# A gate table in DRAM, filled by indexed DMA and read back, in place of one-hot matmuls

## The chip, the cores and the metric

One core of a Trainium2 chip runs the kernel as one program. The metric is the device time of an execution in microseconds (us). The engines work side by side: TensorE (PE, matrix products), VectorE (DVE), ScalarE (ACT), GpSimd (POOL) and SyncE (SP, which here starts most DMAs). Each takes its instructions in one fixed order, and an instruction that waits holds up all that are queued behind it on its engine.

## The reference

Two transformer blocks over 256 tokens of width 2048, in float32. The part around the change is the expert layer (PEER) of the first block. Each token picks, for each of 8 heads, 16 of 16384 experts by two searches over 128 keys each, and every expert has a row `u` and a row `v`:

```python
s = jnp.einsum('thpd,hpnd->thpn', q, sub_keys)
s_half, i_half = lax.top_k(s, PEER_TOPK)                  # 16 of 128, twice per head
cand = s_half[:, :, 0, :, None] + s_half[:, :, 1, None, :]
cand_idx = i_half[:, :, 0, :, None] * PEER_NKEYS + i_half[:, :, 1, None, :]
top_s, pos = lax.top_k(cand, PEER_TOPK)                   # 16 of 256
idx = jnp.take_along_axis(cand_idx, pos, axis=-1)
g = jax.nn.softmax(top_s, axis=-1)
...
a = jnp.einsum('cd,ced->ce', xc, expert_u[ic])
w = (gc * jax.nn.gelu(a)).astype(xc.dtype)
y = jnp.einsum('ce,ced->cd', w, expert_v[ic])
```

So a token has 8 x 16 = 128 picks (with repetitions over the heads, whose gates add up).

## The kernel before

Rather than gather `u`, the kernel computes a token's product with all experts, in 128 blocks of 128 experts, and multiplies by a table of gates that is zero where an expert isn't picked. `w0` and `w1` hold, for each block, 128 experts by 256 tokens. Every float32 product is split in a high and a low part, and three products of the halves are summed.

`stat_block` (L905) is one block: two units of 512 KB (`raw`, loaded by SP), each split by ACT into `hi` (L155) and by DVE into `lo` (L157), and on PE one 512-column matmul (L915, the last one of the block L918) and one of 256 columns (L916) for each of 16 steps. ACT copies half of the result (`rest`, L923), DVE adds it (L924). `raw`, `hi` and `lo` have three buffers each. DVE's order holds the `lo`s between its other work.

`route` (L1204) runs 16 such blocks over the query weights, and behind each the searches (`top16`, L927) on DVE: MAX8, FIND_INDEX8 and MATCH_REPLACE8 over 128 columns for both halves of the tokens, and behind every second block over 256 columns of `cand` (L1233). In between `renorm` scales the input for the expert blocks in four parts: `rn` on POOL (L1198) and DVE (L1199), `xt` on DVE (L1201). Then it works out the two indices and the gate of each pick and transposes them with six PE transposes (L1269 to L1271) into `i1T`, `i2T` and `gT`.

`peer_blocks` (L937) runs the 128 expert blocks. The first 25 (NPARK) only store gelu of the product. In the next 64 each block carries four tokens' gates: `onehots` (L975, L978, DVE) makes for each token two one-hot matrices, one with the gates in it, and a fp32 matmul of the two (L1019, PE) gives the token's 128 x 128 table. `place` multiplies it into the blocks that are done (L991) and stores it for the others (L993), `note` marks the experts in use, and `finish` multiplies a later block by its gates. Then `rank` numbers the experts in use, and the 127 sends of L1034 (indirect DMA, POOL) write the used rows in a compact list, from which `peer_v` gathers `v` (L1159, POOL).

A tile framework sorts every engine's instructions by priority when the program is made; its order is fixed then. A DMA that POOL starts uses one of eight lanes in turn, and waits for the one eight before it.

## Time and profile before

| | |
|---|---|
| median of three runs | 3036.33 us (3036.22 to 3039.43) |
| profiled execution | 3041.31 us, its span 3039.6 us |
| granted TensorE clock, mean | 0.99 |
| busy, share of the span | PE 98%, DVE 67%, ACT 51%, POOL 13% |
| the expert layer's first product | about 419 to 1190 us of the span |

A share of busy time is a mean over the whole span, so the stages have to be read one by one. Where a group of rows is a timeline, its columns are start (us), duration (us), engine, line, operation, what is written and read, and in brackets the idle time before it and what ended that. A row of the windows view gives a stretch, its length, the busy time of PE, PEld (weight loads), DVE, ACT and POOL (with the number of their instructions), the granted TensorE clock as a share of full speed, the DMA engines' busy share and GB/s.

### The profile page before, as it was taken

The numbers are of one execution on the slowest core, as the hardware profiler recorded it, in microseconds if no ns is written. First come the engines' busy times: TensorE is split into PE (matmuls) and PEld (weight loads), VectorE is DVE, ScalarE is ACT, GpSimd is POOL, SyncE is SP. The second block draws the span as 40 slices with busy tenths as digits, with TensorE's granted clock in tenths as the row PEclk, the third lists the DMA queues.
The fourth block names the chain that finished last, engine by engine and source line by source line (L and its number), as shares of the span: only waits on it lengthen the run. The fifth ranks groups of instructions, "written<-read, shape, count | busy, mean of one in ns | idle before, by whom it ended". The sixth has DMA issues, their size and how long they took to land.

```text
span 3039.6 us, 42009 instructions
## 1 busy us (share of the span) xinstructions
PE 2977.8 (98%) x15470; PEld 2522.4 (83%) x15471; DVE 2021.4 (67%) x3213; ACT 1552.3 (51%) x2409; POOL 393.3 (13%) x403
## 2 busy tenths in 40 slices
PE   8999999999999999998998999999999999999998
PEld 6877888888888887887886888888887888888887
DVE  7776899888888555665667644555656555555555
ACT  5555655454554444565666444555445544444444
POOL 3130102100000674221221000000120000000000
PEclk9999999999999999999999999999999999999999
DMA  6434555544444898876887555555574555555554
GB/s 204 149 132 143 190 188 175 172 166 161 162 164 167 257 285 263 287 285 249 289 293 268 181 192 181 173 170 182 171 243 158 189 191 188 190 192 194 194 194 166
DMA packets 168502, 607.88 MB, mean 200 GB/s; under 512 B 20672, under 2 KB 36096, under 8 KB 154464
## 3 DMA queue, kind: packets, MB, share of 16 engines
q1 hardware_dynamic: 142272, 461.95, 45.2%
q0 software_dynamic: 26016, 143.17, 13.0%
q8 instruction: 123, 2.02, 0.3%
q14 instruction: 91, 0.75, 0.1%
HBM read 581.96 MB, written 23.07 MB: 199 GB/s over the span
## 4 chain that ended last, share of the span: by engine, by line
PE 45%; issue 4%; DMA 1%; POOL 1%; DVE 1%; ACT 0%; POOLq 0%; DVEq 0%; ACTq 0%; SPq 0%
PE mm L915 7%; PE mm L181 7%; PE mm L180 7%; PE mm L182 7%; PE mm L916 4%; PE mm L1107 2%; PE mm L1109 2%; PE mm L1108 2%; POOL vr L1159 1%; PE at L1109 1%; PE at L1107 1%; PE tr L1107 1%; PE at L1108 1%; PE tr L1109 1%; PE tr L1108 1%
## 5 line engine op out<-in xcount | busy, mean ns | idle before, releaser
L157 DVE TENSOR_TENSOR lo<-raw,hi 128x1024 fp32r<-128x1024 f32 (+2 forms) x852 | 1047.7, 1230 | 558.8 <-ACT hi L155 555.7
L155 ACT ACTIVATE hi<-raw 128x1024 fp32r<-128x1024 f32 (+2 forms) x852 | 894.1, 1050 | 624.0 <-PE mm L182 265.0
L915 PE MATMUL mm<-xt,hi 128*128 128x512 f32 x3120 | 1124.9, 399 | 1.1 <-DVE xt L205 1.1
L916 PE MATMUL mm<-xt,lo 128*128 128x256 f32 x3328 | 904.0, 282 | 5.2 <-DVE lo L157 5.1
L915 PEld LDWEIGHTS mm<-xt,hi 128*128 128x128 f32 x3120 | 587.5, 188 | 113.9 <-DVE xt L205 1.5
L916 PEld LDWEIGHTS mm<-xt,lo 128*128 128x128 f32 x3328 | 628.8, 189 | 22.4 <-DVE lo L157 7.6
L181 PE MATMUL mm<-lo,xt 128*128 128x512 f32 (+2 forms) x928 | 363.3, 392 | 0.3 <-DVE lo L157 0.2
L182 PE MATMUL mm<-hi,xt 128*128 128x512 f32 (+2 forms) x928 | 356.1, 387 | 0.0
L157 DVE TENSOR_TENSOR lo<-vr,hi 128x1024 fp32r<-128x1024 f32 x206 | 253.4, 1235 | 137.8 <-ACT hi L155 132.6
L180 PE MATMUL mm<-hi,xt 128*128 128x512 f32 (+2 forms) x928 | 335.0, 391 | 4.9 <-ACT hi L155 2.8
L155 ACT ACTIVATE hi<-vr 128x1024 fp32r<-128x1024 f32 x206 | 216.3, 1055 | 143.8 <-PE mm L1109 122.2
L923 ACT ACTIVATE rest<-mm 128x256 f32<-128x256 f32 x208 | 80.0, 385 | 368.7 <-PE mm L918 368.6
L1108 PE MATMUL mm<-lo,wh 128*128 128x512 f32 x560 | 219.0, 391 | 0.0
L1109 PE MATMUL mm<-hi,wl 128*128 128x512 f32 x560 | 218.6, 391 | 0.0
L180 PEld LDWEIGHTS mm<-hi,xt 128*128 128x128 f32 x928 | 174.9, 190 | 40.4 <-ACT hi L155 3.4
L181 PEld LDWEIGHTS mm<-lo,xt 128*128 128x128 f32 x928 | 176.3, 190 | 35.5 <-DVE lo L157 2.0
L182 PEld LDWEIGHTS mm<-hi,xt 128*128 128x128 f32 x928 | 175.7, 190 | 32.8 <-DVE xt L205 0.4
L1107 PE MATMUL mm<-hi,wh 128*128 128x512 f32 x560 | 157.9, 394 | 15.7 <-ACT hi L155 13.4
L924 DVE TENSOR_TENSOR mm<-mm,rest 128x256 f32<-128x256 f32 x208 | 88.8, 427 | 95.3 <-ACT rest L923 95.2
L1034 POOL DMA_INDIRECT wD<-w,rank x127 | 137.9, 1086 | 77.9 <-DVE bad L1092 21.0
L1159 POOL DMA_INDIRECT vr<-in_peer_v,wr x103 | 96.7, 939 | 329.5 <-DVE lo L157 295.5
L1107 PEld LDWEIGHTS mm<-hi,wh 128*128 128x128 f32 x560 | 105.6, 190 | 39.8 <-ACT hi L155 15.7
(484 smaller groups left out, 3700.9 us busy)
## 6 DMA issues: line engine op xcount, KB each, us to landing
raw<-in_peer_u SPq DMA_DIRECT2D x256, 512.0 KB, 3.3
raw<-in_w_in SPq DMA_DIRECT2D x184, 512.0 KB, 3.2
raw<-in_w_up SPq DMA_DIRECT2D x128, 512.0 KB, 3.2
raw<-in_w_down SPq DMA_DIRECT2D x128, 512.0 KB, 3.5
raw<-in_w_out SPq DMA_DIRECT2D x64, 512.0 KB, 3.3
raw<-in_peer_w_q SPq DMA_DIRECT2D x32, 512.0 KB, 3.5
wr<-wD SPq DMA_DIRECT2D x103, 128.5 KB, 3.5
raw<-in_w_branch_a SPq DMA_DIRECT2D x16, 512.0 KB, 3.2
```

The source lines that it names most:

```text
L155: nc.scalar.activation(hi[:, :n], raw[:, :n], AF.Copy)
L157: nc.vector.tensor_tensor(lo[:, :n], raw[:, :n], hi[:, :n].bitcast(F32), op=ALU.subtract)
L180: mm(o, sh, wh, start=(k == 0), stop=False)
L181: mm(o, sh, wl, start=False, stop=False)
L182: mm(o, sl, wh, start=False, stop=(k == nk - 1))
L915: mm(out, wh, x.both(k), start=(k == 0), stop=False)
L916: mm(out[:, S:], wl, x.hi(k), start=False, stop=False)
L1034: nc.gpsimd.indirect_dma_start(lots[b], bass.IndirectOffsetOnAxis(ap=rank[:, b:b + 1], axis=0), store(b, b + 1)[:, 0, :], None)
L1107: mm(o, sh, vh, start=first, stop=False)
L1108: mm(o, sh, vl, start=False, stop=False)
L1109: mm(o, sl, vh, start=False, stop=last)
L1159: nc.gpsimd.indirect_dma_start(v, None, a["peer_v"], bass.IndirectOffsetOnAxis(ap=w[:, S:ROW].bitcast(U32), axis=0))
```

## The change

The gates go through a table `gD` in DRAM, of 128 blocks x 128 experts x 256 tokens. At the route's start POOL clears it with 16 DMAs of 1 MB from a zeroed part of `w0`. The picks stay with the tokens on the partitions (`eid`, `gate`), so the transposes fall away. For every pick p, DVE sums the gates of all picks of the token with the same expert (`gates`: one operation over 128 x 128 with a sum), and POOL writes the 128 sums of the 128 tokens with one indirect DMA to their cells (128 rows of 4 bytes; a repeated pick goes to a spare block): 2 x 128 indirect DMAs. When all are written, POOL fetches the table into the tiles: blocks 80 to 111 (LATE to RING) into their own place by 8 DMAs of 512 KB, the blocks that are done by DMAs of 256 KB (two blocks) into the free place of blocks 112 to 127, eight at a time. The done blocks are multiplied there in pairs, on POOL or DVE, and `used` finds the experts in use by a maximum on DVE or by sums on ACT. Blocks 25 to 79 store gelu alone, the later ones multiply in `finish`.

```diff
-TPB = 4
-USE = 16
+PICKS = 6
+MARK = 16.0
+GATED = 76
+LATE = 80
+RING = 112
...
-            i1T = gp.tile([P, S], F32, name="i1T")
-            i2T = gp.tile([P, S], BF16, name="i2T")
-            gT = gp.tile([P, S], F32, name="gT")
-            um = gp.tile([P, N0], F32, name="um")
+            eid = gp.tile([P, 2, P], F32, name="eid")
+            gate = gp.tile([P, 2, P], F32, name="gate")
...
-            def onehots(gw):
...
-            def place(blk, ps):
...
-            def note():
...
+            spots = dram_disjoint_views(self.gD, 2 * P)
+            blocks = self.gD[:NBLK * P * S].rearrange("(b p s) o -> b p (s o)", p=P, s=S)
+            todo = [(t, p) for t in range(2) for p in range(0, P, PICKS)]
...
+            def gates():
+                t, p0 = todo.pop(0)
+                ps = range(p0, min(p0 + PICKS, P))
+                for p in ps:
+                    nc.vector.scalar_tensor_tensor(same, ids2[t][:, p:p + P], eid[:, t, p:p + 1], gate2[t][:, p:p + P],
+                                                   op0=ALU.is_equal, op1=ALU.mult, accum_out=total[:, t, p:p + 1])
+                sl = slice(p0, ps.stop)
+                nc.vector.scalar_tensor_tensor(skip[:, t, sl], total[:, t, sl], MARK, skip[:, t, sl],
+                                               op0=ALU.is_ge, op1=ALU.mult)
+                nc.vector.tensor_tensor(place[:, t, sl], cell[:, t, sl], skip[:, t, sl], op=ALU.add)
+                for p in ps:
+                    nc.gpsimd.indirect_dma_start(spots[t * P + p],
+                                                 bass.IndirectOffsetOnAxis(ap=place[:, t, p:p + 1], axis=0),
+                                                 total[:, t, p:p + 1], None)
+
+            def used(v, b, act):
+                if act:
+                    for i in range(2):
+                        for t in range(2):
+                            j = self.junk.tile([P, P], BF16, name="junk", tag="rest", bufs=2)
+                            nc.scalar.activation(j, v[:, i, t * P:(t + 1) * P], AF.Copy,
+                                                 accum_out=um[:, t, b + i:b + i + 1])
+                    return
+                nc.vector.tensor_reduce(um[:, :, b:b + 2], v.rearrange("p b (t s) -> p t b s", t=2), axis=AX.X, op=ALU.max)
 
...
             blk = NPARK
-            with tc.tile_pool(name="gw", bufs=4, reuse_waits="tile") as gw:
-                while done < S:
-                    gps = self.bank("at")
-                    oh = onehots(gw)
-                    def fill(i):
-                        nc.tensor.matmul(gps[:, i * P:(i + 1) * P], oh[i][0], oh[i][1], start=True, stop=True)
-                    ps = self.stat_block(x, a["peer_u"][blk], fill=fill)
-                    place(blk, gps)
-                    if done % USE == 0:
-                        note()
-                    finish(blk, ps)
-                    blk += 1
+            def block():
+                nonlocal blk
+                finish(blk, self.stat_block(x, a["peer_u"][blk]))
+                blk += 1
+            with tc.tile_pool(name="gw", bufs=1, reuse_waits="tile") as gw:
+                um = gw.tile([P, 2, NBLK], F32, name="um")
+                pairs()
+                while todo:
+                    gates()
+                    block()
+                def fetch(b, n, at):
+                    nc.gpsimd.dma_start(store(at, at + n)[:, :, :S], blocks[b:b + n].rearrange("b p s -> p b s"))
+                for b in range(LATE, RING, 4):
+                    fetch(b, 4, b)
+                early = list(range(0, LATE, 2))
+                late = list(range(LATE, NBLK, 2))
+                got, slot = [], RING
+                def load():
+                    nonlocal slot
+                    for _ in range(3):
+                        if early:
+                            b = early.pop(0)
+                            fetch(b, 2, slot)
+                            got.append((b, slot))
+                            slot = slot + 2 if slot + 2 < NBLK else RING
+                load()
+                while blk < GATED:
+                    block()
+                while got or late:
+                    now = list(got)
+                    got.clear()
+                    if early:
+                        load()
+                    for i, (b, at) in enumerate(now):
+                        sv, g = store(b, b + 2)[:, :, :S], store(at, at + 2)[:, :, :S]
+                        (nc.vector if i == 1 else nc.gpsimd).tensor_tensor(sv, sv, g, op=ALU.mult)
+                        used(g, b, i == 1)
+                    if now and not got:
+                        for b in range(RING, NBLK, 4):
+                            fetch(b, 4, b)
+                    for i in range(1 if now else 3):
+                        if late:
+                            b = late.pop(0)
+                            used(store(b, b + 2)[:, :, :S], b, i == 0)
+                    block()
+                nc.vector.tensor_scalar(use[:, :, :NR], um[:, :, :NR], 0.0, None, op0=ALU.is_gt)
...
+        self.gD = self.dram.tile([(NBLK + 1) * P * S, 1], F32, name="gD")
+        zero = w0[:, N0 - 8:N0].rearrange("p b s -> p (b s)")[:, :D]
+        nc.gpsimd.memset(zero, 0.0)
+        clear = self.gD[:NBLK * P * S].rearrange("(i p f) o -> i p (f o)", p=P, f=D)
...
         for cb in range(16):
+            nc.gpsimd.dma_start(clear[cb], zero)
...
-        tr = self.bank("tr")
-        tr2 = self.bank("tr")
         for t in range(2):
-            nc.tensor.transpose(tr[:, t * P:(t + 1) * P], ii[:, t, 0], self.ident)
-            nc.tensor.transpose(tr[:, 256 + t * P:256 + (t + 1) * P], ii[:, t, 1], self.ident)
-            nc.tensor.transpose(tr2[:, t * P:(t + 1) * P], gs[:, t].rearrange("p h k -> p (h k)"), self.ident)
-        nc.vector.tensor_copy(i1T, tr[:, 0:256])
-        nc.vector.tensor_copy(i2T, tr[:, 256:512])
-        nc.vector.tensor_copy(gT, tr2[:, 0:256])
+            nc.vector.scalar_tensor_tensor(eid[:, t], ii[:, t, 0], float(P), ii[:, t, 1], op0=ALU.mult, op1=ALU.add)
```

The change moves instructions on DVE and POOL. First DVE at the route's start: MAX, MAX_INDEX and MATCH_REPLACE are the searches (`sv`, `si` over keys, `cs`, `cp` over `cand`), and `rn`, `xt` the renormalization. Before, these rows stand there:

```order
L157 TENSOR_TENSOR lo<-raw,hi 128x1024
L934 MAX sv<-t16w 128x8
L1199 TENSOR_TENSOR rn<-rn,r2row 128x1024
L931 MAX sv<-scr 128x8 x2
L935 MAX_INDEX si<-sv,t16w 128x8
L157 TENSOR_TENSOR lo<-raw,hi 128x1024
L932 MAX_INDEX si<-sv,scr 128x8 x2
L933 MATCH_REPLACE t16w<-sv,scr 128x128
```

The two `lo`s are the 91st and the 92nd. In the changed kernel this stands on DVE ahead of the 92nd, whose line is now L160:

```order
L934 MAX cs<-cand 128x8
L935 MAX_INDEX si<-sv,scr 128x8 x2
L937 MAX cs<-t16w 128x8
L935 MAX_INDEX cp<-cs,cand 128x8
L938 MAX_INDEX cp<-cs,t16w 128x8
L1249 TENSOR_TENSOR rn<-rn,r2row 128x1024
L936 MATCH_REPLACE t16w<-cs,cand 128x256
L937 MAX cs<-t16w 128x8
L938 MAX_INDEX cp<-cs,t16w 128x8
L1251 TENSOR_TENSOR xt_3237<-rn,xt_3237 128x4x256
L936 MATCH_REPLACE t16w<-sv,scr 128x128
L160 TENSOR_TENSOR lo<-raw,hi 128x1024
```

So the searches over `cand`, and the second `rn`, have come ahead of `lo`s that they followed. On POOL, from the first `rn` to the first product, the changed program has (`w_3226` is `w0`, `w_5855` is `w1`):

```order
L1267 DMA gD<-w_3226 128x2048 x16
L1248 TENSOR_TENSOR rn<-xt_2815 128x1024
L1248 TENSOR_TENSOR rn<-xt_2816 128x1024
L1248 TENSOR_TENSOR rn<-xt_2817 128x1024
...
L1003 DMA gD<-w_5855 4227072x1 x256
L1039 DMA w_5855<-gD 128x4x256 x8
L1039 DMA w_5855<-gD 128x2x256 x8
L1066 TENSOR_TENSOR w_3226<-w_3226,w_5855 128x2x256
```

The 16 clears stand ahead of the second, third and fourth `rn`, and behind the 256 scatters the eight fetches of four blocks ahead of the eight of two. On DVE, where the first fetched pairs are used, the changed program has:

```order
L927 TENSOR_TENSOR mm<-mm,rest 128x256
L1015 TENSOR_REDUCE um<-w_5855 128x2x2 x2
L1066 TENSOR_TENSOR w_3226<-w_3226,w_5855 128x2x256
L160 TENSOR_TENSOR lo<-raw,hi 128x1024
L1015 TENSOR_REDUCE um<-w_5855 128x2x2 x2
L1066 TENSOR_TENSOR w_3226<-w_3226,w_5855 128x2x256
```

The maximum (L1015) and the product (L1066), which need a fetched pair, stand ahead of the 264th `lo`; before, one-hots (L975, L978) stood in their place.

## Rows read from the trace of the kernel before

**Rows 1.** The page: engines' busy time; bytes moved in 40 slices.

```profile
PE 2977.8 (98%) x15470; PEld 2522.4 (83%) x15471; DVE 2021.4 (67%) x3213; ACT 1552.3 (51%) x2409; POOL 393.3 (13%) x403
...
GB/s 204 149 132 143 190 188 175 172 166 161 162 164 167 257 285 263 287 285 249 289 293 268 181 192 181 173 170 182 171 243 158 189 191 188 190 192 194 194 194 166
```

**Rows 2.** Windows view: route's searches, and the one-hot stage.

```profile
380.00:505.00 125.00, 125.00 (x732) 110.49 (x731) 122.14 (x392) 65.36 (x106) 0.00 (x0) 1.00 0.55 188
...
567.00:972.00 405.00, 405.00 (x2515) 363.20 (x2514) 349.82 (x767) 204.00 (x415) 0.00 (x0) 1.00 0.48 165
```

**Rows 3.** PE timeline: the L918 of single blocks.

```profile
480.84 0.40 PE L918 MATMUL mm<-xt,hi 128*128 128x512 f32 x1
...
486.41 0.40 PE L918 MATMUL mm<-xt,hi 128*128 128x512 f32 x1
...
539.41 0.40 PE L918 MATMUL mm<-xt,hi 128*128 128x512 f32 x1
...
549.47 0.39 PE L918 MATMUL mm<-xt,hi 128*128 128x512 f32 x1
...
560.73 0.40 PE L918 MATMUL mm<-xt,hi 128*128 128x512 f32 x1
...
978.15 0.39 PE L918 MATMUL mm<-xt,hi 128*128 128x512 f32 x1
```

**Rows 4.** Windows view, same columns, at the transposes.

```profile
543.00:547.00 4.00, 4.00 (x15) 3.43 (x15) 4.00 (x6) 0.44 (x2) 1.96 (x2) 0.57 0.63 231
```

**Rows 5.** DVE timeline at the route's start.

```profile
340.50 2.13 DVE L157 TENSOR_TENSOR lo<-raw,hi 128x1024 fp32r<-128x1024 f32 x1
...
351.95 1.20 DVE L157 TENSOR_TENSOR lo<-raw,hi 128x1024 fp32r<-128x1024 f32 x1
```

**Rows 6.** Lines view, DVE, 335 to 560 us: busy us, mean ns.

```profile
L932 DVE FIND_INDEX8 si<-sv,scr 128x8 uint32<-128x128 f32 x32 | 8.8, 282 | 0.0
...
L932 DVE FIND_INDEX8 cp<-cs,cand 128x8 uint32<-128x256 f32 x16 | 6.7, 417 | 0.0
...
L978 DVE TENSOR_SCALAR o<-iota,i1T,gT 128x128 f32<-128x128 f32 x1 | 0.3, 335 | 0.0
```

**Rows 7.** POOL timeline: the second `rn`.

```profile
339.15 2.40 POOL L1198 TENSOR_TENSOR rn<-xt 128x1024 f32<-128x1024 f32 x1 [9.60 <-DVE xt L1201]
```

**Rows 8.** POOL timeline: sends of L1034.

```profile
1000.99 2.04 POOL L1034 DMA_INDIRECT wD<-w,rank  x1 [21.03 <-DVE bad L1092]
...
1006.14 0.96 POOL L1034 DMA_INDIRECT wD<-w,rank  x1 [0.30 <-ACT hi L155]
...
1009.94 1.46 POOL L1034 DMA_INDIRECT wD<-w,rank  x1 [0.30 <-ACT mm L1009]
...
1139.74 0.96 POOL L1034 DMA_INDIRECT wD<-w,rank  x1 [0.30 <-issue]
```

**Rows 9.** POOL timeline: a gather of L1159.

```profile
1204.15 0.95 POOL L1159 DMA_INDIRECT vr<-in_peer_v,wr  x1 [0.30 <-issue]
```

**Rows 10.** DVE timeline beside those sends.

```profile
1009.34 1.23 DVE L157 TENSOR_TENSOR lo<-raw,hi 128x1024 fp32r<-128x1024 f32 x1 [0.51 <-ACT hi L155]
```

**Rows 11.** DMA view: issues, and us to landing.

```profile
wD<-w,rank POOLq DMA_INDIRECT x127, 5.6
```

**Rows 12.** Lines view, POOL: a plain DMA's issue.

```profile
L564 POOL DMA_DIRECT2D hD<-hr x8 | 4.4, 553 | 42.8 <-DVE hr L562 42.6
```

**Rows 13.** POOL timeline: products of 128x512.

```profile
513.16 1.29 POOL L1264 TENSOR_TENSOR oneh<-oneh,sif 128x512 f32<-128x512 f32 x1 [3.65 <-DVE oneh L1259]
516.61 2.15 POOL L1264 TENSOR_TENSOR oneh<-oneh,sif 128x512 f32<-128x512 f32 x1 [2.16 <-DVE oneh L1259]
```

**Rows 14.** The page: costliest groups, two of ACT.

```profile
L155 ACT ACTIVATE hi<-raw 128x1024 fp32r<-128x1024 f32 (+2 forms) x852 | 894.1, 1050 | 624.0 <-PE mm L182 265.0
...
L923 ACT ACTIVATE rest<-mm 128x256 f32<-128x256 f32 x208 | 80.0, 385 | 368.7 <-PE mm L918 368.6
```

**Rows 15.** The page: the software DMA queue.

```profile
q0 software_dynamic: 26016, 143.17, 13.0%
```

More of the change, by code (lines that the diff above doesn't have):

```diff
@@ L65 @@
 SB = 4
-PAD_XN = 32
+PAD_XN = 288
 SWA_ACT = (0,)
@@ L950, in peer_blocks @@
             with tc.tile_pool(name="rt", bufs=1, reuse_waits="tile") as rt:
-                self.route(rt, x, i1T, i2T, gT)
+                self.route(rt, x, eid, gate, w0)
                 for blk in range(NPARK):
@@ L983, in place @@
-            def place(blk, ps):
-                nonlocal done
-                pv = ps.rearrange("p (t i) -> p i t", t=TPB)
-                ts = slice(done, done + TPB)
-                for b0, b1 in ((0, N0), (N0, NBLK)):
-                    m = min(max(blk, b0), b1)
-                    if m > b0:
-                        sv = store(b0, m)[:, :, ts]
-                        nc.vector.tensor_tensor(sv, pv[:, b0:m], sv, op=ALU.mult)
-                    if m < b1:
-                        nc.scalar.activation(store(m, b1)[:, :, ts], pv[:, m:b1], AF.Copy)
-                done += TPB
@@ L996, in note @@
-            def note():
-                t = (done - USE) // P
-                for b0, b1 in ((0, N0), (N0, NR)):
-                    u = use[:, t, b0:b1]
-                    m = um[:, :b1 - b0]
-                    nc.vector.tensor_reduce(m, store(b0, b1)[:, :, done - USE:done], axis=AX.X, op=ALU.max,
-                                            apply_absolute_value=True)
-                    nc.vector.scalar_tensor_tensor(u, m, 0.0, u, op0=ALU.is_gt, op1=ALU.max)
+            sent = 0
+            spots = dram_disjoint_views(self.gD, 2 * P)
@@ new lines, in peer_blocks @@
+            blocks = self.gD[:NBLK * P * S].rearrange("(b p s) o -> b p (s o)", p=P, s=S)
+            todo = [(t, p) for t in range(2) for p in range(0, P, PICKS)]
+            spare = [store(b, b + 1)[:, 0, :S] for b in range(RING, NBLK)]
+            ids2, gate2 = spare[0:2], spare[2:4]
+            cell, skip, total = (v.rearrange("p (t k) -> p t k", t=2) for v in spare[4:7])
+            place, same = spare[7].bitcast(U32).rearrange("p (t k) -> p t k", t=2), spare[8][:, :P]
+            tok = us.tile([P, 2, 2], F32, name="tok")
@@ new lines, in peer_blocks, with pairs @@
+            for i in range(2):
+                nc.gpsimd.iota(tok[:, i], pattern=[[P, 2]], base=i * NBLK * P * S, channel_multiplier=1,
+                               allow_small_or_imprecise_dtypes=True)
+            def pairs():
+                for t in range(2):
+                    for i in range(2):
+                        h = slice(i * P, (i + 1) * P)
+                        nc.vector.tensor_copy(ids2[t][:, h], eid[:, t])
+                        nc.vector.tensor_scalar(gate2[t][:, h], gate[:, t], MARK * i, None, op0=ALU.add)
+                    nc.vector.tensor_scalar(cell[:, t], eid[:, t], float(S), tok[:, 0, t:t + 1], op0=ALU.mult, op1=ALU.add)
+                    nc.vector.tensor_scalar(skip[:, t], self.iota, float(S), tok[:, 1, t:t + 1], op0=ALU.mult, op1=ALU.add)
+                    nc.vector.tensor_tensor(skip[:, t], skip[:, t], cell[:, t], op=ALU.subtract)
@@ new lines, in used @@
+            def used(v, b, act):
+                if act:
+                    for i in range(2):
+                        for t in range(2):
+                            j = self.junk.tile([P, P], BF16, name="junk", tag="rest", bufs=2)
[3 more added lines that the diff above has]
+                nc.vector.tensor_reduce(um[:, :, b:b + 2], v.rearrange("p b (t s) -> p t b s", t=2), axis=AX.X, op=ALU.max)
@@ L1201, in renorm, with route @@
             nc.vector.tensor_tensor(x.part(i, 1), v, x.part(i, 0).bitcast(F32), op=ALU.subtract)
-    def route(self, rt, x, i1T, i2T, gT):
+    def route(self, rt, x, eid, gate, w0):
         nc, a = self.nc, self.a
+        self.gD = self.dram.tile([(NBLK + 1) * P * S, 1], F32, name="gD")
+        zero = w0[:, N0 - 8:N0].rearrange("p b s -> p (b s)")[:, :D]
+        nc.gpsimd.memset(zero, 0.0)
+        clear = self.gD[:NBLK * P * S].rearrange("(i p f) o -> i p (f o)", p=P, f=D)
         s2 = rt.tile([P, 2], F32, name="s2")
@@ L1244, in route @@
         nc.vector.tensor_copy(af[:, 1], ab)
-        gs = rt.tile([P, 2, 8, 16], F32, name="gsm")
+        gs = gate.rearrange("p t (h k) -> p t h k", h=8)
         zs = rt.tile([P, 16], F32, name="zs")
```

25 lines of the change are left out of this document (5 added, 20 removed).

## Prediction

> **What bounds the kernel now.** I read the page first: its table of engines puts TensorE (PE) at 98% of the span, VectorE (DVE) at 67% and GpSimd (POOL) at 13% [rows 1]. So work taken from PE shortens the time one for one, and work added elsewhere costs only where it makes PE wait. Then I cut the stretch that the change touches into stages with the windows view [rows 2]. From 380 to 505 us PE is busy throughout and DVE for 122.14 of 125 us: the top-16 searches leave DVE no room, so a `lo` that falls behind there is not caught up. From 567 to 972 us (the one-hot stage) PE is busy for all 405 us, DVE for 349.82, POOL not at all. Last, the PE timeline gives the price of a block, since each block has one L918 matmul, at its end [rows 3]: 480.84 to 486.41 is 5.57 us without one-hots.
>
> **Removed: the one-hot matmuls.** From the L918 at 560.73 to that at 978.15 lie 65 blocks [rows 3], 417.4 us or 6.42 each. At 5.567 they would take 361.9, so the one-hots cost 55.5 us, in 64 blocks. Term: **−55.5**. At the route's end the block from 539.41 to 549.47 takes 10.06 us instead of 5.57 [rows 3]; it holds the six transposes, which wait for DVE, and from 543 to 547 us the granted clock is 0.57 [rows 4]. The three blocks up to 560.73 take 21.3 us instead of 16.7. Term: **−4.6**, bounds 0 (DVE is as late without the transposes) and −4.6.
>
> **Moved: the route's start.** In the changed order the top-16 work of the first blocks stands on DVE ahead of `lo`s that stood before it. Over four `lo`s (before, the first runs at 340.50 and the fourth at 351.95 [rows 5]) the old order has 8.4 us of other DVE work and the new one 30.1, by operations of known cost: a 128-wide search takes 0.28 us and, overlapped, 0.20 from start to start, a 256-wide one up to 0.42 [rows 6], an `rn` or `xt` as long as an undisturbed `lo`, 1.20 [rows 5]. Besides, POOL now issues 16 clears of 1 MB ahead of the second `rn`, and a software DMA waits for the one eight before it. No slice of this trace moves more than 293 GB/s [rows 1], so the first eight, 8.4 MB, take up to 29 us; POOL is free for them at 329.55, 9.60 us ahead of the second `rn` of before at 339.15 [rows 7], which would now start some 20 us later. DVE's own `rn` line waits for POOL's, `lo`s are queued behind it, and PE eats those, with three buffers as the only cover. Walking both orders with these durations puts the fourth `lo` 27 to 36 us later; thinner DVE work behind it gives some 3 back. Below, if the clears land in time, the searches alone: 30.1 − 8.4 = 21.7, less two ready `lo`s of half a block (2.78), 16. Term **R = +27**, bounds 16 and 35.
>
> **Added: 256 scatters.** An indirect DMA of 4 bytes per row is not in the trace. The nearest rows are the 127 sends of L1034 (128 rows of 1028 bytes) and the gathers of L1159 (8 KB rows): 0.96 and 0.95 us, with 0.30 us of "issue" between two [rows 8, 9]. Eight times the bytes change nothing, so the cost is per row, and 4 bytes should cost the same. The first send starts at 1000.99, the 101st at 1139.74 [rows 8]: **c = 1.39 us** each. The floor is 0.96 + 0.30, with rounding 1.27. The rest is contention with DVE: the send at 1009.94 starts inside the `lo` of 1009.34, which ends at 1010.57, and takes 1.46 us, half a microsecond more than the usual 0.96 [rows 8, 10].
> The Trainium skill ("SBUF — State Buffer", the section on its two sides) says that a DVE operation with two SBUF inputs and a GpSimd one lock each other out of a shared port for a whole instruction. The rows agree with that; with the lock c is 1.39, without it 1.27.
>
> The scatters keep POOL for 256 × 1.39 = 356 us. The first stands just ahead of the 155th `lo` of the DVE order (the fourth of above is the 94th), the first use of a fetched gate (line 1015 of the changed kernel, on DVE) 109 `lo`s later, that is 109 × 2.783 = 303 us. A fetch waits for all scatters, and on DVE the `lo`s stand behind line 1015, so PE stops. Behind the last scatter come its landing (5.6 us for a send from its issue [rows 11], some 4 beyond POOL's part) and the fetches, where eight of 512 KB for blocks not yet due stand ahead of the first of 256 KB that is: 4.5 MB, 15 us at 293 GB/s, 16 with an issue of 0.55 [rows 12]. So 356 + 20 − 303 = 73, less 5 for ready `lo`s. Term **S = +68**, bounds 37 (c = 1.27) and 96 (c = 1.5, were nearly every send as slow as the one of 1.46). S is nothing at c = 1.125 or less.
>
> A rule speaks against the change. The Trainium skill ("DMA: Bandwidth & Descriptors", rules for kernel authors) says that below 64 KB a transfer is mostly overhead and that many small ones belong in one large; its section on latency puts the fixed cost at about 2 us. As an estimate from that page 256 in series take 512 us, and the time would be some 156 us above my sum. The sends here, 1.39 apart though 5.6 in landing, overlap, so no trace here bears a series out.
>
> **Added: the multiplications.** 40 products of 128x512 go to POOL (27) and DVE (13), with eight sums of 128x128 per block on ACT. A POOL product of that size takes 1.29 us alone and 2.15 beside DVE [rows 13]: 35 to 58 us, with 40 fetch issues of 0.55 (22 us) [rows 12] 57 to 80, against 12 blocks = 67 us. ACT has two `hi` of 1.05, a `rest` of 0.385, a gelu like it and eight sums, as an estimate like `rest` too [rows 14]: 5.95 us per block against 5.57. The clock is low after PE waited [rows 4], too. Term **M = +10**, bounds 0 and 20. The sends behind need 127 × 1.39 = 176.5 us and have 33 blocks × 5.57 = 184: nothing. DVE's six picks per block, about 0.34 each by the one-hot of L978 [rows 6], are 2 us and take the place of four L978 and more: hidden.
>
> **Sum.** The profiled execution took 3041.3 us (span 3039.6): 3041.3 − 55.5 − 4.6 + 27 + 68 + 10 = 3086.2. It lies 5 above the median of the three runs, so 3081, rounded to **3080 us**.
>
> **Rivals.** (B, the other side) A scatter's issue is shorter than a send's because its payload is 4 bytes, towards the 0.55 of a plain DMA [rows 12]. From c = 1.125 down the table is there before it is needed, S is 0 and the time 3041.3 − 60.1 + 27 + 10 − 5 = 3013; with R gone as well, 2986. Against it: 0.95 for 8 KB rows beside 0.96 for 1 KB. (C) The small packets bind the DMA engines. The software queue's 26016 packets took 13.0% of 16 engines' span [rows 15], 0.243 us each; 32768 would take 498 us on 16 engines, so c = 1.94, S 141 more, 3221. Most of those packets were far larger than 4 bytes, so this is a ceiling. (D) R and M cost nothing: the searches are only moved, and POOL has room. Then 3041.3 − 60.1 + 68 − 5 = 3044, slower by 0.3%; about 0.2% (6 us) is what a measurement of this kernel can tell from no change. With c = 1.27 it is 3013.
>
> **How the numbers follow.** Forecast 0.57; D, or a time between it and the forecast, 0.16, of which 0.05 within 0.2% and 0.02 faster; B 0.20, a quarter of it without R; C 0.07. That is faster 0.22, same 0.05, slower 0.73. The likeliest case's own range is 3045 to 3110 (c from 1.27 to 1.5, R from 16 to 35, M from 0 to 20, not all at one end). To leave out no more than 2 in 10, the range takes in B with R: 3005 to 3112.
>
> **What would show it.** Right: blocks of 5.57 us between L918s once the picks run; on POOL 256 indirect DMAs 1.3 to 1.5 us apart; then DVE idle at line 1015 for some 70 us, PE idle with it, and a low granted clock behind; and a gap of 15 to 35 us in PE between 340 and 375 us. Wrong: scatters 1.1 us apart or less, or POOL waiting for DMAs between them; a second `rn` on POOL that starts near 339; or blocks well above 5.57 us all through the picks, which would make DVE the bound there.

## The result, and the profile after

The changed kernel takes 3125.62 us (median of four runs, 3122.61 to 3133.33) against 3036.27 for the kernel before on the same chip (3035.88 to 3039.43): a ratio of 1.0288, interval 1.0275 to 1.0301. It is slower, by twice what was predicted. The profiled execution has a span of 3120.9 us, 81.3 above that of before; the ledger below goes by these two spans.

The page of the changed kernel, against [rows 1]: PE has 47 us less work, POOL is busy for 772 us instead of 393, and the span grew, so PE now waits. In the costliest groups stands the scatter, L1003, with its mean and the idle time ahead of it.

```profile
span 3120.9 us, 41529 instructions
...
PE 2930.3 (94%) x14953; PEld 2466.1 (79%) x14953; DVE 1977.0 (63%) x3282; ACT 1553.2 (50%) x2491; POOL 771.6 (25%) x757
...
L1003 POOL DMA_INDIRECT gD<-w x256 | 289.3, 1130 | 87.1 <-issue 72.2
```

The windows view of the changed kernel: the stretch, its length, the busy time of PE, weight loads, DVE, ACT and POOL, the granted clock, the share of the DMA engines, GB/s.

```profile
342.00:392.00 50.00, 21.10 (x76) 16.34 (x77) 39.11 (x121) 12.20 (x20) 11.11 (x9) 0.63 0.79 318
...
567.00:871.00 304.00, 304.00 (x1749) 268.00 (x1749) 238.50 (x746) 144.79 (x218) 241.22 (x207) 1.00 0.67 190
871.00:960.00 89.00, 3.97 (x22) 3.27 (x21) 7.82 (x7) 2.66 (x4) 64.04 (x70) 0.53 0.25 78
960.00:972.00 12.00, 9.28 (x37) 7.40 (x36) 12.00 (x11) 3.21 (x5) 8.65 (x9) 0.76 0.56 176
```

PE is starved twice: from 342 to 392 us, beside a DVE that is busy, and from 871 to 960 us, beside a DVE that is idle and a POOL that is not. Between the two it stands for less than 3 us.

**The route's start.** POOL's timeline, the 16 clears (L1267) and the second `rn`; eight are issued in a row, and each further one waits for one to land:

```profile
325.98 4.25 POOL L1267 DMA_DIRECT2D gD<-w  x8
330.93 0.53 POOL L1267 DMA_DIRECT2D gD<-w  x1 [0.70 <-DMA gD<-w]
334.98 0.53 POOL L1267 DMA_DIRECT2D gD<-w  x1 [3.52 <-DMA gD<-w]
...
356.53 0.53 POOL L1267 DMA_DIRECT2D gD<-w  x1 [2.12 <-DMA gD<-w]
357.08 2.35 POOL L1248 TENSOR_TENSOR rn<-xt 128x1024 f32<-128x1024 f32 x1
```

DVE's timeline at the same place. The `lo`s of 346.65, 363.38, 371.82 and 386.22 are the 91st to the 94th, those that ran from 340.50 to 351.95 in [rows 5]:

```profile
346.65 1.20 DVE L160 TENSOR_TENSOR lo<-raw,hi 128x1024 fp32r<-128x1024 f32 x1
...
359.46 1.23 DVE L1249 TENSOR_TENSOR rn<-rn,r2row 128x1024 f32<-128x1024 f32 x1 [7.93 <-POOL rn L1248]
...
363.38 3.32 DVE L160 TENSOR_TENSOR lo<-raw,hi 128x1024 fp32r<-128x1024 f32 x1
...
371.82 1.21 DVE L160 TENSOR_TENSOR lo<-raw,hi 128x1024 fp32r<-128x1024 f32 x1
...
386.22 3.48 DVE L160 TENSOR_TENSOR lo<-raw,hi 128x1024 fp32r<-128x1024 f32 x3
```

The second `rn` starts 17.9 us after that of [rows 7]; DVE stands 7.93 us for it and works through searches for the rest. The fourth `lo` is 34.3 us late, 37.7 if one allows that this execution is 3.4 ahead at its start (the ledger below). The clears also hold up the raw loads: the five that SP issued from 327.0 to 347.9 took 9 to 13 us to their last packet, where the median of this run is 3.5, and ACT, and with it DVE, waits for one of them:

```profile
336.66 1.06 ACT L158 ACTIVATE hi<-raw 128x1024 fp32r<-128x1024 f32 x1 [5.40 <-DMA raw<-in_peer_w_q]
```

So three things make the fourth `lo` late. In the order, 33.6 us of other DVE work stand between the 90th and the 94th instead of 8.6 (25.0 more); DVE stands 7.9 us for POOL's `rn`; and just ahead of these it stands 4.6 us for the late load. Together that is 37.5. PE's two longest waits:

```profile
362.78 0.80 PE L918 MATMUL mm<-xt,hi 128*128 128x512 f32 x1 [10.01 <-ACT hi L158]
...
387.48 0.58 PE L919 MATMUL mm<-xt,lo 128*128 128x256 f32 x1 [6.46 <-DVE lo L160]
```

**The table.** POOL's timeline at the end of the scatters: they are 1.27 us apart here, then come the fetches (L1039) and the first product.

```profile
930.24 0.96 POOL L1003 DMA_INDIRECT gD<-w  x1 [0.30 <-issue]
931.51 0.96 POOL L1003 DMA_INDIRECT gD<-w  x1 [0.30 <-issue]
932.78 0.97 POOL L1003 DMA_INDIRECT gD<-w  x1 [0.30 <-issue]
935.45 6.06 POOL L1039 DMA_DIRECT2D w<-gD  x8 [1.70 <-issue]
...
953.47 1.28 POOL L1066 TENSOR_TENSOR w<-w,w 128x512 f32<-128x512 f32 x1
```

The first scatter starts at 566.70, the last at 932.78: 366.1 us, over 255 steps 1.436 each. DVE meets the first use of a fetched gate (L1015) long before that and waits; the `lo` that PE wants is behind it:

```profile
952.48 1.44 DVE L1015 TENSOR_REDUCE um<-w 128x4 f32<-128x512 f32 x2 [80.12 <-DMA w<-gD]
953.99 1.32 DVE L1066 TENSOR_TENSOR w<-w,w 128x512 f32<-128x512 f32 x1
955.23 4.17 DVE L160 TENSOR_TENSOR lo<-raw,hi 128x1024 fp32r<-128x1024 f32 x1
```

On PE's timeline this is one wait, in a block whose end (L921 is each block's last matmul here) comes 92.2 us after the one before:

```profile
871.01 0.40 PE L921 MATMUL mm<-xt,hi 128*128 128x512 f32 x1
...
959.46 0.58 PE L919 MATMUL mm<-xt,lo 128*128 128x256 f32 x1 [85.03 <-DVE lo L160]
...
963.21 0.40 PE L921 MATMUL mm<-xt,hi 128*128 128x512 f32 x1
```

**The ledger.** Counted block by block, by how much later a block's last matmul starts than in the kernel before. Blocks 0 to 127 are the experts', 16 blocks of the route stand ahead of them.

| stretch | later at its end, us | change in it | predicted |
| --- | --- | --- | --- |
| up to the route's fourth block | −3.4 | −3.4 | 0 |
| route's start (R) | +33.4 at block 0 | +36.8 | +27 |
| route's end | +31.9 at block 23 | −1.5 | −4.6 |
| blocks 25 to 88 without one-hots | | −55.5 | −55.5 |
| the wait at block 74 (S) | +75.2 at block 74 | +86.6 | +68 |
| products and what follows (M) | +78.6 at block 127 | +15.6 | +10 |
| behind the blocks | +81.3 at the end | +2.7 | 0 |

From block 23 to 73 the kernel gains 42.4 us (31.9 to −10.5); the kernel before has some 49 one-hot fillings there, so one is worth 0.87 us, and a block takes 5.57 us. The −55.5 is this price for all 64. S is the step from block 73, 85.7, with the 0.87 that this block saves too. M is 14 blocks at 0.87 that gained 2.6 instead of 12.2, and 6.0 more by block 127. The lead of 3.4 at the start lies ahead of all that was changed; over the runs below it is 1 to 6.

### The profile page after: what moved, and what is told of

It is laid out like the page before. It is cut to its first block, busy times and chain, and to the rows that moved or that the text cites. A ratio compares the mean times of both kernels' runs of the same rounds, so it can differ in the third digit from the quotient of the medians.

```text
span 3120.9 us, 41529 instructions
## 1 busy us (share of the span) xinstructions
PE 2930.3 (94%) x14953; PEld 2466.1 (79%) x14953; DVE 1977.0 (63%) x3282; ACT 1553.2 (50%) x2491; POOL 771.6 (25%) x757
## 4 chain that ended last, share of the span: by engine, by line
PE 44%; issue 4%; DMA 1%; POOL 1%; DVE 1%; ACT 0%; POOLq 0%; DVEq 0%; SPq 0%; ACTq 0%
PE mm L918 7%; PE mm L184 7%; PE mm L183 7%; PE mm L185 7%; PE mm L919 4%; PE mm L1159 2%; PE mm L1158 2%; PE mm L1157 2%; POOL vr L1209 1%; PE tr L1157 1%; PE tr L1158 1%; PE at L1159 1%; PE at L1157 1%; PE tr L1159 1%; PE at L1158 1%
## 5 line engine op out<-in xcount | busy, mean ns | idle before, releaser
L160 DVE TENSOR_TENSOR lo<-raw,hi 128x1024 fp32r<-128x1024 f32 (+2 forms) x852 | 1063.9, 1249 | 610.4 <-ACT hi L158 608.0
L918 PE MATMUL mm<-xt,hi 128*128 128x512 f32 x3120 | 1107.2, 395 | 14.5 <-ACT hi L158 13.4
L918 PEld LDWEIGHTS mm<-xt,hi 128*128 128x128 f32 x3120 | 591.4, 190 | 135.7 <-ACT hi L158 13.9
L160 DVE TENSOR_TENSOR lo<-vr,hi 128x1024 fp32r<-128x1024 f32 x206 | 253.2, 1235 | 138.0 <-ACT hi L158 133.1
L1003 POOL DMA_INDIRECT gD<-w x256 | 289.3, 1130 | 87.1 <-issue 72.2
L1159 PE MATMUL mm<-hi,wl 128*128 128x512 f32 x560 | 217.5, 389 | 0.0
## 6 DMA issues: line engine op xcount, KB each, us to landing
gD<-w POOLq DMA_DIRECT2D x16, 1024.0 KB, 20.3
```

What stands on the lines that cost most here:

```text
L160: nc.vector.tensor_tensor(lo[:, :n], raw[:, :n], hi[:, :n].bitcast(F32), op=ALU.subtract)
L918: mm(out, wh, x.both(k), start=(k == 0), stop=False)
L1003: nc.gpsimd.indirect_dma_start(spots[t * P + p], bass.IndirectOffsetOnAxis(ap=place[:, t, p:p + 1], axis=0), total[:, t, p:p + 1], None)
L1159: mm(o, sl, vh, start=False, stop=last)
```

## Experiments

Two theories stood after the result. **A (terms apart)**: R and S are two waits with causes of their own, and without the one the time falls by its size. **P (one chain)**: the table is a chain, from the picks to the last send, and it is longer than what PE has left to do, so removing R or moving the wait of S only moves the idle time. In the profile the chain is 366.1 us of scatters, 19.7 of landing and fetching, 143.1 of products, late blocks and rank, 183.6 of sends: 712.5 us from 566.70 to the last send's start. The scatters and sends are POOL's; in the 143.1 us between, POOL is busy for 65 only, and at their end it waits for DVE, which ranks:

```profile
1082.73 0.36 POOL L1108 TENSOR_SCALAR_AFFINE_SELECT tri<-tri 128x128 bf16<-128x128 bf16 x1 [30.36 <-DVE tri L1107]
1095.58 1.96 POOL L1084 DMA_INDIRECT wD<-w,rank  x1 [12.48 <-DVE bad L1142]
...
1279.15 0.97 POOL L1084 DMA_INDIRECT wD<-w,rank  x1 [0.30 <-issue]
1285.97 0.99 POOL L1209 DMA_INDIRECT vr<-in_peer_v,wr  x1 [5.84 <-DMA wr<-wD]
```

PE's last block ends at 1275.85, and from 566.70 on PE has 709 us, 622 without the wait of 86.6. About R there was a rival too: **T**, that it is the traffic of the 16 MB, not the place in POOL's order.

Each kernel was timed in three rounds against the kernel before on the same chip. Three groups of runs fell on chips on which the kernel before itself takes 3141 to 3148 us; their totals are not set beside the others, and the same kernels ran again where it takes 3038 to 3040.

**1. Half of the scatters (half).** Every odd pick is not written, so half of the gates are missing from the output.

```diff
+                    if p % 2:
+                        continue
                     nc.gpsimd.indirect_dma_start(spots[t * P + p],
```

> Only the scatters of the even picks are issued, 128 of 256; half of the gates are left out of the table, all else stays. Theory A (the stall of 86 us before block 73 is the length of the scatter train): 128 x 1.44 = 184 us end long before the first use, the stall goes to nothing and the time to 3126 - 86 = about 3037 to 3040. Rival L (the fetches behind the last scatter, their landing, or the products are what DVE waits for at block 73): the scatters end 180 us earlier but 20 us or more of stall stay, 3060 or more.

3054.0 us, ratio 1.0048 (1.0031 to 1.0064), against 3039.26 for the kernel before. That lies between the two forecasts. The scatters run from 566.7 to 771.9, 1.62 apart, beside a DVE that is busy for 187 of 203 us. The wait shrinks from 86.6 us to 12 and 5 in blocks 60 and 61, so most of S is the scatters' length. At block 127 the kernel is 2.9 us behind the kernel before, at the end 11.2, since PE then waits for the sends.

**2. A later due block (gated_92).** The constant that says after which block the products begin.

```diff
-GATED = 76
+GATED = 92
```

> The first products are put 16 blocks (89 us) later by GATED = 92 instead of 76, with the same scatters. Theory A alone (only the place of the wait is wrong): the stall of 86 us goes, about 3040. Theory P (POOL's chain of scatters, fetches, products and sends is as long as what PE has left, so that what is saved at the wait comes back behind the last block): the stall at the first use goes, but rank and the 127 sends start 16 blocks later in the program, some 90 us of sends lie behind the last expert block, and the time stays at 3105 to 3130.

3201.95 us, 1.0529 (1.0501 to 1.0558), outside both forecasts: the edit did not do what it was meant to, and the run doesn't decide between A and P. The wait did not move: block 74, as long as before (90.87 us after the block ahead, from 874.05). The order on DVE shows why: the first fetched gate's maximum still stands behind 263 `lo`s. The framework puts the instruction where it plans it; here the place of the line in the loops did not count, as no data held it back. What moved is the rest: the first send comes at 1181.6 instead of 1095.6, PE's last block ends at 1272.1, and the retrieve waits for the sends:

```profile
1368.14 0.80 PE L1157 MATMUL mm<-hi,wh 128*128 128x512 f32 x1 [86.45 <-ACT hi L158]
```

**3. The clears behind the `rn`s, in a row (clear_dep).** A small subtraction over `xt` makes them depend on the last renormalization.

```diff
-            nc.gpsimd.dma_start(clear[cb], zero)
...
+                v = x.part(3, 1).bitcast(F32)[:, 0, :P]
+                nc.gpsimd.tensor_tensor(zero[:, :P], v, v, op=ALU.subtract)
+                for i in range(16):
+                    nc.gpsimd.dma_start(clear[i], zero)
```

> The 16 clears are the same DMAs on the same queue, but read a source whose first 128 columns POOL writes from the last normalized part, so they can start only behind the fourth rn. Theory A (the loss at the route's start, 42 us by the L918/L921 pairs, is the queue: rn waits on POOL behind the clears, and the order that was made for that): nearly all of it goes, 3126 - 35 to 42 = about 3084 to 3091. Rival T (the 16.8 MB of clears slow the raw loads, wherever they stand): the loss moves a few blocks on and at least 20 us of it stay, 3105 or more.

3130.9 us, 1.0302 (1.0284 to 1.0319). The second `rn` starts at 337.00, so the wait for it is gone, yet as much is lost a few blocks later: the kernel is 2.8 us ahead at the route's eighth block, 10.2 behind at the eleventh and 35.8 at the fourteenth. The windows, ACT's wait for a raw load, the last clear, and PE's longest wait there:

```profile
370.00:400.00 30.00, 22.18 (x104) 17.79 (x102) 25.81 (x107) 7.06 (x17) 6.76 (x13) 0.83 1.02 410
400.00:432.00 32.00, 12.33 (x41) 9.74 (x42) 27.64 (x111) 5.99 (x10) 0.25 (x1) 0.62 0.74 297
...
377.76 1.06 ACT L158 ACTIVATE hi<-raw 128x1024 fp32r<-128x1024 f32 x1 [5.07 <-DMA raw<-in_peer_w_q]
...
397.61 0.53 POOL L1286 DMA_DIRECT2D gD<-w  x1 [2.25 <-DMA gD<-w]
...
426.66 0.58 PE L919 MATMUL mm<-xt,lo 128*128 128x256 f32 x1 [13.51 <-DVE lo L160]
```

The last clear is issued at 397.61 and the clears' packets move until 420, so most of both windows lies beside them: PE loses 8 of the first 30 us and 20 of the next 32. That a loss follows the clears is T's forecast, and A's failed. But the traffic is the smaller part of it. The raw loads issued from 369.0 to 407.6 take 8 to 15 us to their last packet, and DVE stands 3.0 us for one (ACT 5.07). What PE waits for is DVE's order: between the 102nd and the 106th `lo` it holds 39.9 us of other work, and 7.3 in the kernel before; DVE is busy for 27.64 of the 32 us. Where the clears stood at first, the order is as before (8.1 us beside the 91st to 94th `lo`). So the order that the framework makes went along with the row of clears.

**4. The clears paced (clear_paced).** Eight of them depend on the scores of one head each, eight on gelu of blocks 0 to 14.

```diff
-            nc.gpsimd.dma_start(clear[cb], zero)
...
+                nc.gpsimd.tensor_tensor(zero[:, :1], sc[:, :1], sc[:, :1], op=ALU.subtract)
+                nc.gpsimd.dma_start(clear[cb // 2], zero)
...
+                        nc.gpsimd.tensor_tensor(self.zero[:, :1], g, g, op=ALU.subtract)
+                        nc.gpsimd.dma_start(self.clear[8 + blk // 2], self.zero)
```

> The same 16 clears one by one: eight behind the searches of every second block of the route, eight behind every second parked block, each held by a one-column POOL write of its source. Theory A: the whole loss at the route's start goes, 3126 - 42 = about 3084, and the second rn starts on POOL near 340 us. Rival T: the same bytes, spread over some 30 blocks, add 1 MB per 11 us to raw loads of 188 GB/s; if loads suffer from any clear, blocks there take over 5.9 us each and 10 us or more stay lost, 3095 or more.

3105.35 us, 1.0211 (1.0194 to 1.0228). R is gone: the kernel is 1.5 us behind at the route's last blocks, 43.6 ahead at block 79, and no raw load beside the clears takes over 7.1 us to its last packet. But the wait of S comes at block 80 and is longer:

```profile
872.00:965.00 93.00, 5.00 (x30) 4.15 (x28) 7.54 (x6) 5.25 (x20) 69.49 (x75) 0.54 0.27 83
...
958.56 1.44 DVE L1019 TENSOR_REDUCE um<-w 128x4 f32<-128x512 f32 x2 [84.77 <-DMA w<-gD]
```

The picks are ready no earlier (scatters from 572.8 to 939.9): DVE is busy for 125.4 of the 130 us up to them (440 to 570). Of the 32 us that the blocks gained at the route, 20 are left in the medians, 15 in the spans. By A it had to be all, so A falls. T's time (3095 or more) was met too, but not its blocks.

**5. One row of clears in the first expert blocks (clear_burst).** All 16 depend on the gelu of block 12, far from the `rn`s.

```diff
-            nc.gpsimd.dma_start(clear[cb], zero)
...
+                    if blk == 12:
+                        g = w0[:, blk, :P]
+                        nc.gpsimd.tensor_tensor(self.zero[:, :P], g, g, op=ALU.subtract)
+                        for i in range(16):
+                            nc.gpsimd.dma_start(self.clear[i], self.zero)
```

> All 16 clears in one row again, but held until parked block 12's result, some 100 us behind the renormalization, when few searches are left on DVE. Theory O (what was lost at the clears was mostly the order of DVE and the wait at rn, not the bytes): blocks 12 to 22 lose less than 8 us more than with paced clears, and the time is within 8 us of 3105. Rival T (a burst of 8 clears in flight starves the raw loads): 13 us or more are lost in blocks 12 to 22.

> The kernel of clear_burst once more, for the same reason. Theory O: blocks 12 to 22 lose less than 8 us more than with paced clears, ratio 1.02 to 1.025. Rival T (a burst of eight clears in flight starves the raw loads): 13 us or more lost there.

On a chip with 3038.3 for the kernel before (clear_burst_c): 3119.22 us, 1.0273 (1.0256 to 1.0290). Blocks 15 to 17 lose 52.7 us, more than R. DVE, ACT and POOL there:

```profile
521.74 0.69 DVE L1325 TENSOR_REDUCE ii<-oneh 128x32 f32<-128x512 f32 x1 [15.00 <-POOL oneh L1324]
...
506.41 1.06 ACT L158 ACTIVATE hi<-raw 128x1024 fp32r<-128x1024 f32 x1 [0.66 <-DMA raw<-in_peer_u]
510.15 1.06 ACT L158 ACTIVATE hi<-raw 128x1024 fp32r<-128x1024 f32 x1 [2.69 <-DMA raw<-in_peer_u]
...
519.88 0.53 POOL L960 DMA_DIRECT2D gD<-w  x1 [1.92 <-DMA gD<-w]
520.43 2.49 POOL L1324 TENSOR_TENSOR oneh<-oneh,sif 128x512 f32<-128x512 f32 x2
```

T's time was met, but by another way: `raw` is waited for 3.4 us in all, at 416 GB/s (500 to 540 us), while DVE stands 15 us for a POOL product that is queued behind the clears. And once more the order went along: between the 147th and the 150th `lo` stand 35.1 us of other DVE work, and 6.1 in the kernel before. Of the loss, DVE's order has the most, then POOL's queue, the traffic a few us.

**6. The wait tied to a block (paced_dep).** With paced clears, the fetches' target is written from a late block's matmul, so that no fetched gate can be planned ahead of it, and the products begin behind block 94 (some blocks fewer are multiplied late).

```diff
-GATED = 76
-LATE = 80
+GATED = 94
+LATE = 98
...
+                while blk < GATED:
+                    last = block()
+                nc.vector.tensor_copy(store(RING, NBLK)[:, :, 0], last[:, :NBLK - RING])
```

> The paced clears, and the products truly put later: the ring's fetches now wait for a small DVE copy of block 93's result (GATED = 94, LATE = 98), so the made order has the first use 43 half-blocks behind that of the run with paced clears alone (306 against 275 lo's at the first maximum, the copy included). Theory A (the 92 us stall before block 80 is a wait in the wrong place): it goes, nothing comes in its stead, 3105 - 92 = about 3013 to 3020. Theory P (POOL's chain from the route's end to the last send is what bounds): the stall shrinks to under 15 us, the last send and the wait behind the last block come later by as much, and the time stays at 3095 to 3130.

> The kernel of paced_dep on another chip. Theory A: ratio to before 0.992 to 0.996. Theory P: the stall under 15 us in blocks 74 to 96, a wait of 70 us or more between the last expert block and the gathers, ratio 1.018 to 1.03.

On a chip with 3040.25 for the kernel before (paced_dep_d): 3109.5 us, 1.0232 (1.0215 to 1.0249). S is as good as gone (DVE waits 5.56 us at L1019), the kernel is 57.8 us ahead at block 92, and PE's last block ends 111 us earlier than in the changed kernel. Then PE waits for the first gather:

```profile
1168.00:1270.00 102.00, 4.84 (x22) 3.65 (x20) 1.27 (x3) 1.25 (x3) 74.21 (x78) 0.54 0.31 108
...
960.99 0.69 DVE L1019 TENSOR_REDUCE um<-w 128x4 f32<-128x512 f32 x1 [5.56 <-DMA w<-gD]
...
1263.01 0.97 POOL L1092 DMA_INDIRECT wD<-w,rank  x1 [0.30 <-issue]
...
1275.53 0.79 PE L1165 MATMUL mm<-hi,wh 128*128 128x512 f32 x1 [102.69 <-ACT hi L158]
```

The scatters run from 568.1 to 941.1, the sends from 1088.8 to 1263.0, and PE's retrieve starts 12.5 us behind the last send, in the changed kernel 13.6. With paced clears alone the last send started at 1260.6: the stall is gone, and the end is where it was (spans of 3105.5 and 3107.4). P had forecast the time and the wait behind the blocks; it had the last send later, and it isn't.

**7. Paced clears and half of the scatters (half_paced).** The two edits of 1 and 4; half of the gates are missing again.

> Paced clears with only the 128 scatters of the even picks; half of the gates are left out of the table. The chain of POOL is 184 us shorter than with all. Theory P: it no longer bounds, so the 37 us of the route's start arrive in full this time (they gave only 20 with all scatters): 3054 - 37 = about 3010 to 3022, faster than before. Rival (the 37 us are lost again to something else, such as DVE): 3030 or more.

> The kernel of half_paced on another chip. Theory P: 3054 - 37 with a few us of a longer stall at the first use, whose place in the order stays put, about 3015 to 3030, ratio 0.992 to 0.998. Rival: ratio above 1.0.

On a chip with 3040.25 (half_paced_b): 3025.94 us, 0.9958 (0.9941 to 0.9974). Where the chain is short (568.3 to 1177.1), most of what removing R gives reaches the end: at block 127 the kernel is 25.0 us ahead where half was 2.9 behind, and the span is 29.6 shorter. A wait of S stays, 18.5 us over blocks 66 and 67 (19.75 and 9.92 us instead of 5.57).

**8. Both ways side by side (hybrid).** A whole computation: the first 128 tokens' gates come from one-hot matmuls (blocks 47 to 78), the other 128 tokens' through a table of half the size (8 paced clears, 128 scatters), with products on POOL behind block 61.

```diff
-GATED = 76
+GATED = 62
+TPB = 4
+USE = 16
...
-            spots = dram_disjoint_views(self.gD, 2 * P)
+            spots = dram_disjoint_views(self.gD, P)
```

> The whole computation, split by tokens: the first 128 tokens keep the one-hot matmuls (in blocks 47 to 78), the other 128 go through a table of half the size (8 paced clears, 128 scatters, products on POOL behind block 61). PE keeps 32 of the 64 fillings. Theory P (POOL's chain of scatters and sends bounds the changed kernel, and not PE): with 184 us taken from the chain it fits beside PE, the stall and the tail go, and half of the one-hots' 55.5 us is gained: 3036 - 28 + 3 to 8 us for the clears and the clock = about 3010 to 3018, ratio 0.992 to 0.995. Rival (a stall of any table read back, whatever its size): ratio above 1.005.

> The kernel of hybrid a third time: in both calls before, the kernel before took over 3140 us, and raw loads stood behind sends and scatters for up to 60 us at a time in both kernels. As there, if the chip does not show that: theory P, ratio to before 0.992 to 0.995; rival, above 1.005.

On a chip with 3038.3 (hybrid_c): 3021.65 us, 0.9944 (0.9927 to 0.9960), faster than both kernels. It is 2.1 us ahead up to block 17, 20.4 at block 54, 13.6 at block 68 where the products start, 21.5 from block 92 on, and PE is at 98% again. POOL's scatters in the page:

```profile
L1002 POOL DMA_INDIRECT gD<-w x128 | 143.7, 1123 | 51.8 <-issue 35.0
```

They run from 571.6 to 753.4, 1.43 apart, and the last send starts at 1173.4: the chain has 601.8 us and hides, as PE's last block ends at 1175.7, behind it.

**9. On the other chips.** The same kernels where the kernel before takes 3141 to 3148 us: half_paced 0.9888 (0.9840 to 0.9936), paced_dep 1.0474, clear_burst 1.0517; hybrid 0.9992 (0.9855 to 1.0130), then paced_dep_b 1.0564 and clear_burst_b 1.0673 beside it; hybrid_b 0.9996 (0.9971 to 1.0021) and paced_dep_c 1.0495. What was written before these repeats:

> The kernel of paced_dep once more, since in that call the kernel before took 3145 us instead of 3036 and raw loads were late in stages that no edit touches. As there. Theory A: ratio to before 0.992 to 0.996. Theory P: stall under 15 us in the blocks 74 to 96, a tail of 70 us or more between the last expert block and the gathers, ratio 1.018 to 1.03.

> The kernel of clear_burst once more, for the same reason. Theory O: blocks 12 to 22 lose less than 8 us more than with paced clears, ratio 1.02 to 1.025. Rival T (a burst of eight clears in flight starves the raw loads): 13 us or more lost there.

> The kernel of hybrid once more, since in that call the kernel before took 3141 us and single raw loads were late by 5 to 30 us in all its later stages. As there: theory P, ratio to before 0.992 to 0.995; rival, above 1.005.

> The kernel of paced_dep a third time, for the same reason. Theory A: ratio to before 0.992 to 0.996. Theory P: the stall under 15 us in blocks 74 to 96, a wait of 70 us or more between the last expert block and the gathers, ratio 1.018 to 1.03.

The signs are those of above but for the hybrid, which is no better than before there. In its run hybrid_b PE starves beside the sends, which are 1.27 us apart; the window, two of PE's matmuls in it, and ACT's wait:

```profile
1075.00:1085.00 10.00, 1.92 (x4) 0.86 (x3) 0.00 (x0) 0.00 (x0) 7.57 (x9) 0.50 0.29 103
...
1081.72 0.59 PE L920 MATMUL mm<-xt,hi 128*128 128x512 f32 x1 [3.13 <-issue]
1084.52 0.37 PE L921 MATMUL mm<-xt,lo 128*128 128x256 f32 x1 [2.21 <-issue]
...
1102.74 1.06 ACT L160 ACTIVATE hi<-raw 128x1024 fp32r<-128x1024 f32 x1 [40.39 <-issue]
```

The expectations above lay this to raw loads that stood behind sends and scatters. The packets do not bear that out: the load that SP issued at 1063.4 was through at 1067.0, and no raw load of hybrid or hybrid_b took over 9.8 us to its last packet. PE itself takes a matmul only every 1.4 to 4.2 us here, and 59.0 us for a block of 32, after idle time that the profile puts down to no releaser ("issue"). On these three chips such idle time of PE is 22 to 177 us per run, in every run on the others 0.2.

## Why the prediction was wrong

The sign was right, both waits came where they were forecast, and the time was missed by 45.6 us, beyond the range's end. The ledger holds 36.4 of them, the span's 81.3 against the sum's 44.9; the rest is that the profiled execution before lay 5 above its median, the one after 3 below, and rounding.

**One-hots (−55.5): right.** From block 23 to 73 a filling gave 0.87 us (42.4 over some 49), where 0.867 were reckoned.

**"Term S = +68": mis-sized, 86.6.** The step that failed first is "**c = 1.39 us** each". The cost per row was right: 0.96 to 0.97 us and 0.30 between two, 4 bytes as dear as the 1028 of [rows 8]. The 48 scatters beside a DVE that stands are 1.27 apart. But the first 208, beside a DVE that works, are 1.47 apart: the picks keep it busier (238.5 of 304 us) than it was beside the sends that gave 1.39 (80.4 of 139 us, 1001 to 1140). The mean is 1.436, and 366.1 us stand where 356 were reckoned. In paced_dep_d, where DVE works on to the end, the last 63 steps are 1.39 each, here 1.30. Second, "less 5 for ready `lo`s": DVE's wait of 80.12 became 86.6 on PE instead of a shorter one, 11.5 more than reckoned, because the maximum, the product and a `lo` of 4.17 us beside POOL's product stand behind it. The rest of the step was as reckoned: landing and fetching took 19.7 for 20, and DVE came to the wait 305.7 us after the first scatter, for 303.

**"Term R = +27": mis-sized, 36.8.** The clears land in 20.3 us, and the second `rn` was 17.9 late, where "some 20" were reckoned. The step that failed is the walk to "27 to 36 us later": the fourth `lo` came 37.7 late. The order cost 25.0 us where 21.7 were reckoned, and the walk had nothing for the raw loads that the clears hold up, 4.6. "Some 3 back" was near: of the 38.8 us that PE had lost at the route's sixth block (−3.4 to +35.4) 2.4 came back by its eleventh. Clear_paced shows that R hangs on the clears' place, and clear_dep and clear_burst_c that it is no matter of that one `rn`: wherever the 16 stand in a row, 37 to 53 us are lost. Most of it is the order on DVE, 25 to 33 us; late loads have some 3 to 5, and waiting for POOL 8 in the changed kernel, 15 or more in clear_burst_c and none in clear_dep.

**The route's end (−4.6): −1.5.** The bound that the text gave as 0 was the better value: without the transposes DVE is nearly as late, with many `lo`s of 1.7 to 2.3 us instead of 1.2 beside POOL's products (503 to 554 us).

**M (+10): 15.6**, in the named bounds. PE's clock is near its lower level, 1.2 GHz, in the wait (0.53) and 0.76 on average up to 972 us, and some of the blocks with products take longer than 5.57 (up to 11.1).

**"The sends behind need 127 × 1.39 = 176.5 us and have 33 blocks × 5.57 = 184: nothing": right to 3 us, but wrong as a balance.** The sends took 183.6, and the retrieve started 3 us late, which is a trifle of the 45.6. But the step set each piece of POOL's work against the blocks beside it, one piece at a time. The chain as a whole, 712 us here, is longer than PE's 622, and the sends end beside the last block only because S had held up the blocks. So R and S are not each worth their size: removing R gave 20 us (clear_paced), removing S as well gave no more (paced_dep_d), and with a short chain the same pacing reached the end (half_paced_b, hybrid_c). The 712 is no fixed length, though. From the first use of a fetched gate to the first send it has 143.1 us here, 116.1 in clear_paced, 127.8 in paced_dep_d and 220 in half. What clear_paced gained at the end is this piece (27 us less), not R; why the planned order made it so is open.

**Rivals.** B (a cheaper scatter) and C (packets bind, 1.94) are out: 1.27 to 1.55 over stretches of 32 scatters. D needed R and M at nothing. The estimate of 512 us, worked out from the Trainium skill's fixed cost of some 2 us ("DMA: Bandwidth & Descriptors", its section on latency) as if the transfers ran in series, isn't borne out: 256 took 366, each 3.5 us in landing (median), so they overlap.

**What stays open.** Why the framework puts other DVE work ahead of the `lo`s beside a row of clears. That it does is shown three times (33.6, 39.9 and 35.1 us where the kernel before has 6 to 9), and that it doesn't where the row is gone: clear_burst_c has 8.1 us beside the 91st to 94th `lo`, the kernel before 8.6. How it plans the clears' time no run shows. Nor does one show how short the piece between the scatters and the sends can be made.

## What to carry to other kernels

Add up the whole chain of the engine that gets the new work, over all stages up to the point where its result is needed, and set that against what the bound engine has left; a stage-by-stage balance finds the waits but not what removing one is worth. Where a framework plans the order, a line's place in a loop or a constant may leave a wait where it was; a data dependency moves it. A row of large DMAs costs more than its own queue: it holds up loads, and the planned order of another engine can change around it, so space the DMAs out and compare the orders. When two engines can do the same work, half on each can beat either, as it did here by 0.6%.

## What the hardware showed that was not expected

An indirect DMA of 128 rows has a floor of 0.94 to 0.97 us of POOL and 0.30 to the next, whether a row has 4, 1028 or 8192 bytes. Beside a row of clears of 1 MB a load of 512 KB takes 8 to 15 us to its last packet instead of 3.5; beside paced ones no load takes over 7.1. On three chips PE stood 22 to 177 us in a run for nothing that the profile shows, DVE 84 to 191; in hybrid_b one block took 59.0 us instead of 5.57, with the DMA engines at 0.29 and 103 GB/s (1075 to 1085 us). In hybrid_c, the same kernel on another chip, no block from the 92nd on lost anything beside the same sends. What sets these chips apart no run here shows.
